# Low parts of the weights made by an accumulating transfer, and used last in a block's first tile and first in its last

## The chip, the cores and the metric

The kernel runs on one core of a Trainium2 chip. The metric is the time on the device in microseconds; lower is better. The engines of a core work side by side: TensorE (matrix products; PE in the profile, PEld for its weight loads), VectorE (DVE), ScalarE (ACT), GpSimd (POOL) and SyncE (SP, which here only issues transfers). Each runs its own instructions in order and waits for the others through semaphores. 16 DMA engines move data between device memory and the on-chip memory.

## The reference

The reference is a decoder trunk of two layers on one sequence of 512 positions with 1024 features, all in float32. A layer normalises x, projects it to all inputs of four mixers, runs the mixers, and adds their projected outputs to x:

```python
# for each of DEPTH = 2 layers, h: (512, 1024)
u = rmsnorm(h, norm_w[l])
z = u @ w_in[l]          # 1024 -> 15 blocks of 512 columns and 16 gate columns
mix = concat(retention(z), diff_attention(z), ssd(z), mlstm(z))   # 4 x 512
h = h + mix @ w_out[l]   # 2048 -> 1024
# at the end
out = rmsnorm(h, final_norm_w)
```

All mixers are causal and work in chunks of 128 positions. What they compute is not touched by the change; the projections' products are the same, the order of their terms in the sum is not.

## The kernel before, in words

**Two parts for each factor.** A product of float32 matrices is made of three products in a narrower format (`fp32r`). Each factor is split: the high part is the value cast to the narrower format, the low part is the value minus the high part. The kernel sums high*high, high*low and low*high. For the activations the parts are `uh` and `ul` (for a mixer's output `mh` and `ml`), for the weights `whi` and `wlo`.

**Tiles and blocks.** The input projection of a layer has 15 blocks of 512 columns, each with 8 pieces of 128 rows (k = 0 to 7). A block has four tiles; each fills one accumulator (`pspj`, of which there are two) with 8 x 3 = 24 matmuls. In `proj_tok` a tile is 128 positions, with the activations as the stationary factor; in `proj_feat` it is 128 features, with the weights stationary. The output projection `out_proj` handles a mixer's 512 rows at a time: two halves of 512 columns with 4 pieces of weights each, four tiles of 12 matmuls a half. A tile's matmuls go by k: the two with the high part of piece k, then the one with its low part.

**How the weights come in.** `split_w` loads two pieces at a time, a pair of 512 KB, into `raw` (two buffers) from SP's queue; `split_half` then casts each piece into `whi` on ScalarE and subtracts, into `wlo`, on GpSimd (pieces k = 0, 2, 4, 6, the tuple `POOL_K`) or on VectorE (the others). `whi` and `wlo` have ten buffers each, one piece a buffer, so a block and two pieces of the next fit. A buffer is free when the last matmul that reads it is done. The instructions of the split have a high priority on their engines (`W["hp"]`).

**Order.** A layer's steps come in this order:

```python
ORDER = ["mv", "gates", "mq", "mk", "mlstm", "mo", "mz", "dk", "dq", "diff", "dv", "dz", "m", "xs", "bc", "ssd", "d",
         "rqk", "sz", "rv", "rz", "ret", "s", "r"]
```

`m`, `d`, `s`, `r` are output projections, `gates`, `mlstm`, `diff`, `ssd`, `ret` the mixers, and all others blocks of the input projection. `gates` and the mixers run as tasks between the projections: `drive` takes the projection's matmuls one by one and, after each `yield`, issues the tasks that have come due on a clock of the TensorE time issued so far (`W` holds the delays). TensorE's order is written out in this way and kept. The other engines' instructions are ordered by a scheduler from priorities, except in the first block (`start`), whose order is written by hand and whose first tile has an order of its own for high and low parts as they come in.

**Around the projections.** A full accumulator is emptied by VectorE and ScalarE: convolution and SiLU (`ev_conv`, L476 to L483), rotation (`ev_rope`, L496 to L500, with a product on GpSimd), SiLU gates (`ev_silu`, L434 and L436), copies, and for the output projections the sum into `h` (L547). `rsqrt` runs on GpSimd (L207). `bcast` (L695) brings rows of the gates to all partitions by transfers from SP's queue. L115 is the line of all matmuls, L316 and L318 those of the cast and the subtraction, L323 that of the load into `raw`.

Of the kernel before, what the change touches and what calls it, by code (L numbers as in the profile page):

```python
# [28 lines left out]
# column offsets of the combined input projection  # L29
# [5 lines left out]
# the 512 column blocks in the order in which they are used  # L35
# [7 lines left out]
# columns of the row parameters that every partition gets  # L43
# [3 lines left out]
# the order of the steps of a layer  # L47
# [3 lines left out]
# the pieces of a block of weights whose low parts GpSimd computes  # L51
POOL_K = (0, 2, 4, 6)

# tiles that hold the queries' parts
QS = 4

# how much work of TensorE is issued before work that depends on other engines
# [5 lines left out]
# columns of the constants  # L63
# [31 lines left out]
class Trunk:  # L95
    def __init__(self, ctx, tc, aps, dbg=None):
        self.tc, self.nc = tc, tc.nc
        self.x, self.win, self.wg, self.wout, self.nrm, self.rows, self.convp, self.cst, self.out = aps
        self.dbg = dbg or {}
        mk = lambda n, b, **k: ctx.enter_context(tc.tile_pool(name=n, bufs=b, **k))  # L100
        self.cp = mk("cp", 1)
        self.pool = mk("pool", 1)
        self.ps = mk("ps", 2, space=bass.MemoryType.PSUM)
        self.n = 0
        # the order of TensorE's work: tasks come due on a clock of emitted TensorE time
        self.clk = 0.0
        self.heap = []
        self.done = set()
# [16 lines left out]
    def spawn(self, gen, delay=0.0):  # L125
        """Runs a generator; what it yields is the delay until it goes on."""
        def step():
            for w in gen:
                self.later(w, step)
                return  # L130
        self.later(delay, step)
# [44 lines left out]
    def setup(self):  # L176
        nc = self.nc
        self.h = [self.cp.tile([P, D], F32, name=f"h{t}") for t in range(NT)]
        for half in range(2):
            hs = slice(half * 512, (half + 1) * 512)  # L180
            nc.sync.dma_start(out=self.h[0][:, hs], in_=self.x[0:P, hs])
        self.load_nw(0, nc.sync)
        cst = self.cp.tile([P, C_W], F32, name="cst")
        nc.sync.dma_start(out=cst[:, 0:P], in_=self.cst[:, 0:P])
        self.rest = lambda: nc.sync.dma_start(out=cst[:, P:], in_=self.cst[:, P:])
        self.c = lambda o, w, p=P: cst[:p, o:o + w]
        self.ident = self.c(C_ID, P)
        self.ones = self.cp.tile([P, P], F32, name="ones")
        nc.vector.memset(self.ones, 1.0)
        # keeps TensorE busy until the first data come in, so that it runs at its full clock  # L190
        p = self.psum()
        for _ in range(12):
            self.mm(p[:, 0:P], lhsT=self.ones, rhs=self.ones)
        self.nhalf = self.cp.tile([P, 8], F32, name="nhalf")
        nc.vector.memset(self.nhalf, -0.5)
        self.zrow = self.cp.tile([4, P], F32, name="zrow")
        nc.vector.memset(self.zrow, 0.0)
# [35 lines left out]
    def load_nw(self, l, eng):  # L233
        """The weights of a norm of h, on every partition."""
        self.nw = [self.t("bcm", [P, 512], bufs=2) for _ in range(2)]
        for half in range(2):
            eng.dma_start(out=self.nw[half],
                          in_=self.nrm[l:l + 1, half * 512:(half + 1) * 512].to_broadcast([P, 512]))
# [72 lines left out]
    def split_half(self, raw, j, vector=False):  # L311
        nc = self.nc
        hi = self.t("whi", [P, 512], F32R, bufs=10)
        lo = self.t("wlo", [P, 512], F32R, bufs=10)
        with self.tc.high_priority(W["hp"]):
            (nc.vector.tensor_copy if vector else nc.scalar.copy)(out=hi, in_=raw)  # L316
            eng = nc.vector if j else nc.gpsimd
            eng.tensor_tensor(out=lo, in0=raw, in1=hi.bitcast(F32), op=ALU.subtract)  # L318
        return hi, lo

    def split_w(self, src, g):
        raw = self.t("raw", [P, 2, 512], bufs=2)
        self.nc.sync.dma_start(out=raw, in_=src)  # L323
        return [self.split_half(raw[:, j, :], 2 * g + j not in POOL_K) for j in range(2)]

    def load_block(self, name):
        b = BIDX[name]
        return [q for g in range(4) for q in self.split_w(self.win[self.l, b, :, 2 * g:2 * g + 2, :], g)]

    def start(self, evac):  # L330
        """The first block: the norm of x, and the weights, as they come in."""
# [9 lines left out]
        with self.tc.manual_schedule(engines={E.Activation, E.DVE, E.Pool, E.SP}):  # L341
# [3 lines left out]
            for k in range(KD):  # L345
                if k < 4:
                    if k % 2 == 0:
                        r = self.t("raw", [P, 2, 512], bufs=2)
                        nc.sync.dma_start(out=r, in_=self.win[0, b, :, k:k + 2, :])
                    raw.append(r[:, k % 2, :])  # L350
                else:
                    raw.append(self.t("z", [P, 512], bufs=8))
                    nc.sync.dma_start(out=raw[k], in_=self.win[0, b, :, k, :])
                if k == 3:
                    load(1)
# [4 lines left out]
            # on VectorE or GpSimd  # L360
            split = lambda k, v, h=False: w.append(self.split_half(raw[k], v, h))
            n = [self.norm_in_t(t) for t in range(NT)]
            # the products with the weights' high parts (0) and low parts (1), as these come in
# [32 lines left out]
    def proj_tok(self, name, evac, w=None, toks=range(NT), order=None):  # L396
        nc = self.nc
        w = w or self.load_block(name)
        for t in toks:
# [4 lines left out]
            for k, parts in order or [(k, (0, 1)) for k in range(KD)]:  # L404
                for part in parts:
                    for u in (self.uh,) if part else (self.uh, self.ul):
                        n += 1
                        self.mm(p, lhsT=u[:, k, ts_], rhs=w[k][part], start=(n == 1), stop=(n == 3 * KD))
                yield
# [3 lines left out]
    def proj_feat(self, name, evac):  # L413
        nc = self.nc
        w = self.load_block(name)
        for f in range(4):
            p = self.psum("pj")
            fs = slice(f * P, (f + 1) * P)
            for k in range(KD):
                hi, lo = w[k][0][:, fs], w[k][1][:, fs]  # L420
                self.mm(p, lhsT=hi, rhs=self.uh[:, k, :], start=(k == 0), stop=False)
                self.mm(p, lhsT=hi, rhs=self.ul[:, k, :], start=False, stop=False)
                self.mm(p, lhsT=lo, rhs=self.uh[:, k, :], start=False, stop=(k == KD - 1))
                yield
            evac(f, p)

    # evacuations
    def ev_silu(self, dst, tag, bufs, nwt=None):
        """2 * silu(z), times a row weight."""
# [57 lines left out]
    def ev_rope(self, sink, scale=1.0):  # L487
        """Rotates the heads' halves; the features lie on the partitions."""
# [21 lines left out]
    def finish_mix(self, mix):  # L510
        """Transposes of a mixer's output, in high and low parts, for the output projection."""
# [8 lines left out]
    def out_proj(self, g, mixt, tok_outer=False, after=None, cut=False, heads=False):  # L520
        nc = self.nc
        gi = GROUPS[g]
        w = [[x for q in range(2) for x in self.split_w(self.wout[self.l, gi, half, :, 2 * q:2 * q + 2, :], 2 * half + q)]
# [4 lines left out]
        for t, hf in order:  # L528
# [5 lines left out]
            for c0, c1 in zip(cuts, cuts[1:]):  # L534
# [4 lines left out]
                for k in range(4):  # L539
                    hi, lo = w[hf][k]  # L540
                    mh, ml = m(t, k)
                    self.mm(p, lhsT=mh, rhs=hi[:, cs], start=(k == 0), stop=False)
                    self.mm(p, lhsT=ml, rhs=hi[:, cs], start=False, stop=False)
                    self.mm(p, lhsT=mh, rhs=lo[:, cs], start=False, stop=(k == 3))
                    yield
# [15 lines left out]
    def gates(self):  # L561
# [20 lines left out]
        # log1p(exp(-|x|)) = 2 atanh(z / (2 + z)), z = exp(-|x|)  # L582
# [31 lines left out]
        # SSD factors  # L614
# [12 lines left out]
        # rows  # L627
# [19 lines left out]
        # running maxima: rows 0.. G, 32.. mu, 64.. G at the end of the chunk  # L647
# [44 lines left out]
    def bcast(self, src, n, t, tag, bufs):  # L692
        """Rows of src, columns of chunk t, on every partition."""
# [9 lines left out]
    def mlstm(self, v, th, zs, q, k, res):  # L703
# [5 lines left out]
        for t in range(NT):  # L709
# [47 lines left out]
            # denominators  # L757
# [18 lines left out]
            # r / 2 * rsqrt(r^2 / 4 * var + eps)  # L776
# [112 lines left out]
    def retention(self, qk, v, zs, res):  # L889
# [6 lines left out]
        for t in range(NT):  # L896
# [6 lines left out]
            # heads on different rows of the array write different banks  # L903
# [55 lines left out]
    def split_k(self, dst):  # L959
        """High and low parts of a head's keys, one above the other, for each of its two maps."""  # L960
# [13 lines left out]
    def split_q(self, x):  # L974
        """The high parts of a head's queries, on both halves of the partitions, and the low parts."""
# [108 lines left out]
    def layer(self, l, last):  # L1084
        """The steps of a layer that keep TensorE busy, and the mixers that run between them."""
# [40 lines left out]
        def end():  # L1126
# [7 lines left out]
            # mLSTM  # L1134
# [8 lines left out]
            # differential attention  # L1143
# [6 lines left out]
            # SSD  # L1150
# [5 lines left out]
            # retention  # L1156
# [7 lines left out]
    # columns of the last tokens' halves  # L1164
# [34 lines left out]
def _layout(i):  # L1199
    """The inputs, cut and reordered into the pieces that the kernel loads."""  # L1200
# [36 lines left out]
```

## Time and profile before

| what | value |
|---|---|
| runs | 1088.46, 1086.24, 1088.56 us; median 1088.46 |
| profiled execution, first to last instruction | 1091.0 us |
| TensorE matmuls | 1043.6 us busy (96%) |
| VectorE / ScalarE / GpSimd | 714.8 / 492.0 / 392.9 us busy |
| granted TensorE clock, mean | 0.984 |
| moved by the DMA engines | 95.53 MB, mean 88 GB/s |

The profile is of one execution; its span is 2.5 us longer than the median of the runs. A row of grouped instructions reads: line, engine, operation, output<-inputs, shapes, count, then busy us and mean ns of one, then the engine's idle time just before them and what ended it. A row of waits reads: who waited, for whom, us in total, times, longest. A row of transfers ends with the size of one and the median us from issue to landing. A row of the timeline reads: start, us, engine (q for its queue), line, operation, tiles, shapes, count, and in brackets the idle time before and what ended it. "Busy" of TensorE counts overlapping, pipelined matmuls once.

### The profile page before, as it was taken

Reading aid. Unit: us, or ns where it says so; the run is one execution under the profiler, and the core shown is the slowest. Engines: PE = TensorE matmul, PEld = TensorE weight load, DVE = VectorE, ACT = ScalarE, POOL = GpSimd, SP = SyncE. Lnnn points to the kernel's source line nnn. Section 1 sums busy time; section 2 is a strip of 40 time slices with the busy share of each in tenths; the row PEclk is TensorE's granted clock in tenths of the full one; section 3 lists DMA queues with packets and bytes.
Section 4 is the critical chain, followed back from the end, with each engine's and each line's share of the span. In section 5 each row is a group of like instructions: output and inputs, shape, how many; then the busy total and the mean of one; then the engine's idle time right before and its main releaser. Section 6 shows DMA issues by size and latency. Waiting matters only on the chain.

```text
span 1091.0 us, 14197 instructions
## 1 busy us (share of the span) xinstructions
PE 1043.6 (96%) x5052; PEld 848.7 (78%) x5052; DVE 714.8 (66%) x1369; ACT 492.0 (45%) x1082; POOL 392.9 (36%) x369
## 2 busy tenths in 40 slices
PE   7999989999999899999999999999999999999997
PEld 6778878777788787787887788787877877787776
DVE  5686676567787767445556867664687886773454
ACT  4444337655554344332344442484555542543332
POOL 3322445324323354225132234533252343542341
PEclk8999999999999999999999999899999999999999
DMA  7332313321312323332122322222231223223202
GB/s 283 102 100 85 97 49 97 96 77 57 92 46 79 106 68 97 108 119 72 39 82 74 116 89 86 78 77 77 79 101 55 78 87 107 71 85 115 78 20 77
DMA packets 39143, 95.53 MB, mean 88 GB/s; under 512 B 3592, under 2 KB 16520, under 8 KB 38944
## 3 DMA queue, kind: packets, MB, share of 16 engines
q1 hardware_dynamic: 38064, 93.18, 26.8%
q10 hardware_dynamic: 1008, 1.44, 0.4%
q8 instruction: 39, 0.64, 0.2%
q14 instruction: 32, 0.26, 0.1%
HBM read 92.47 MB, written 2.15 MB: 87 GB/s over the span
## 4 chain that ended last, share of the span: by engine, by line
PE 79%; DVE 11%; DMA 3%; issue 3%; ACT 3%; POOL 1%; SPq 0%; ACTq 0%; POOLq 0%; DVEq 0%
PE pspj L115 64%; PE psacc L115 6%; PE psS L115 5%; PE psS L119 4%; DVE wlo L318 3%; DMA raw<-in_w_in_dram 2%; DVE w L826 2%; DVE e L478 1%; ACT whi L316 1%; DMA cst<-in_consts_dram 1%; DVE w L721 0%; ACT e L496 0%; POOL s L207 0%; DVE z L436 0%; DVE ft L498 0%
## 5 line engine op out<-in xcount | busy, mean ns | idle before, releaser
L318 POOL TENSOR_TENSOR wlo<-raw,whi 128x512 fp32r<-128x512 f32 x150 | 206.5, 1380 | 358.8 <-ACT whi L316 231.7
L318 DVE TENSOR_TENSOR wlo<-raw,whi 128x512 fp32r<-128x512 f32 x150 | 173.7, 1159 | 89.4 <-ACT whi L316 76.9
L115 PE MATMUL pspj<-whi,uh 128*128 128x512 f32 x512 | 209.5, 409 | 8.5 <-DVE ft L498 8.2
L316 ACT CAST whi<-raw 128x512 fp32r<-128x512 f32 x300 | 175.8, 619 | 91.9 <-DMA raw<-in_w_in_dram 54.7
L115 PE MATMUL pspj<-whi,ul 128*128 128x512 f32 x512 | 201.8, 394 | 0.0
L115 PE MATMUL pspj<-wlo,uh 128*128 128x512 f32 x512 | 201.5, 395 | 0.2
L115 PE MATMUL pspj<-uh,whi 128*128 128x512 f32 x448 | 182.0, 406 | 9.3 <-DVE e L478 4.9
L115 PE MATMUL pspj<-uh,wlo 128*128 128x512 f32 x448 | 177.3, 396 | 1.2 <-POOL wlo L318 1.2
L115 PE MATMUL pspj<-ul,whi 128*128 128x512 f32 x448 | 176.4, 394 | 0.0
L115 PEld LDWEIGHTS pspj<-whi,uh 128*128 128x128 f32 x512 | 97.6, 191 | 31.0 <-DVE ft L498 9.7
L115 PE MATMUL pspj<-whi,mh 128*128 128x512 f32 (+1 forms) x260 | 107.4, 413 | 10.7 <-DVE h L547 8.0
L115 PEld LDWEIGHTS pspj<-wlo,uh 128*128 128x128 f32 x512 | 96.9, 190 | 22.7 <-DVE wlo L318 1.0
L115 PEld LDWEIGHTS pspj<-whi,ul 128*128 128x128 f32 x512 | 97.8, 191 | 18.2 <-DVE ul L306 0.2
L115 PEld LDWEIGHTS pspj<-uh,whi 128*128 128x128 f32 x448 | 85.6, 191 | 28.9 <-issue 6.1
L115 PE MATMUL pspj<-whi,ml 128*128 128x512 f32 (+1 forms) x260 | 102.2, 393 | 0.0
L115 PE MATMUL pspj<-wlo,mh 128*128 128x512 f32 (+1 forms) x260 | 102.2, 393 | 0.0
L115 PEld LDWEIGHTS pspj<-uh,wlo 128*128 128x128 f32 x448 | 85.4, 191 | 21.1 <-POOL wlo L318 2.5
L115 PEld LDWEIGHTS pspj<-ul,whi 128*128 128x128 f32 x448 | 85.6, 191 | 16.2
L207 POOL TENSOR_TENSOR s<-s,nhalf 128x4 f32<-128x4 f32 (+1 forms) x44 | 36.8, 837 | 160.2 <-DVE s L1058 76.0
L478 DVE SCALAR_TENSOR_TENSOR e<-pspj,cvh,e 128x511 f32<-128x511 f32 (+2 forms) x90 | 66.9, 744 | 14.6 <-ACT e L476 13.5
L115 PEld LDWEIGHTS pspj<-whi,mh 128*128 128x128 f32 x260 | 49.4, 190 | 23.7 <-DVE h L547 10.0
L496 ACT ACTIVATE e<-pspj 32x512 f32<-32x512 f32 x96 | 56.6, 590 | 12.9 <-PE pspj L115 11.4
(213 smaller groups left out, 1490.5 us busy)
## 6 DMA issues: line engine op xcount, KB each, us to landing
raw<-in_w_in_dram SPq DMA_DIRECT2D x118, 512.0 KB, 3.9
raw<-in_w_out_dram SPq DMA_DIRECT2D x32, 512.0 KB, 3.3
bcm<-adr SPq DMA_DIRECT2D x16, 256.0 KB, 3.4
bcm<-gdr SPq DMA_DIRECT2D x8, 256.0 KB, 4.9
out_dram<-z SPq DMA_DIRECT2D x7, 256.0 KB, 2.0
h<-in_x_dram SPq DMA_DIRECT2D x3, 512.0 KB, 8.5
rows<-in_rows_dram SPq DMA_DIRECT2D x2, 592.0 KB, 9.0
cst<-in_consts_dram SPq DMA_DIRECT2D x1, 1035.0 KB, 8.9
```

Source lines behind the costliest of these rows:

```text
L115: self.nc.tensor.matmul(out, lhsT=lhsT, rhs=rhs, start=start, stop=stop, **kw)
L119: self.nc.tensor.transpose(out, src, self.ident if ident is None else ident)
L207: self.nc.gpsimd.tensor_tensor(out=out, in0=m, in1=self.nhalf[:, :n], op=ALU.pow)
L316: (nc.vector.tensor_copy if vector else nc.scalar.copy)(out=hi, in_=raw)
L318: eng.tensor_tensor(out=lo, in0=raw, in1=hi.bitcast(F32), op=ALU.subtract)
L478: nc.vector.scalar_tensor_tensor(acc[:, s:], p[:, 0:S - s], w[:, 3 - s:4 - s], acc[:, s:], ALU.mult, ALU.add)
L496: nc.scalar.activation(x[q * 32:q * 32 + 32, :], p[o * 32:o * 32 + 32, :], AF.Copy, scale=scale)
L826: nc.vector.scalar_tensor_tensor(e[:, j * P:(j + 1) * P], ab[g][:, j, :], self.ncs[:, t, h:h + 1], self.cap, ALU.add, ALU.min)
```

## The change

Outside the first block, `split_w` makes both pieces of a pair at once, in tiles `whi` and `wlo` of two pieces with five buffers each (`WP`). ScalarE casts the pair into the high part in one instruction. VectorE no longer subtracts: it writes the negative of `raw`, in the narrower format, into `wlo`. Then GpSimd issues a transfer that reads the same weights from device memory a second time and adds them onto `wlo`. What results is the weights minus their value in the narrower format, the low part as before. GpSimd computes no low parts here any more.

The order of the terms changes in a block's first and last tile (for the output projections, in a half's): the first uses all high parts first and then all low parts, the last all low parts and then all high parts. The tiles between go piece by piece as before.

In the first block the split stays as it was (`split_half`, now writing into slices of pairs), and the first four pieces are loaded singly into buffers of another tag (`ft`) instead of in pairs into `raw`. All other lines of the diff remove comments.

```diff
-POOL_K = (0, 2, 4, 6)
+WP = 5, 5
+
+def parts(n, first, last):
+    hi, lo = [[(k, (j,)) for k in range(n)] for j in range(2)]
+    return hi + lo if first else lo + hi if last else [(k, (0, 1)) for k in range(n)]
...
-    def split_half(self, raw, j, vector=False):
-        nc = self.nc
-        hi = self.t("whi", [P, 512], F32R, bufs=10)
-        lo = self.t("wlo", [P, 512], F32R, bufs=10)
+    def pair(self):
+        return [self.t(tag, [P, 2, 512], F32R, bufs=n) for tag, n in zip(("whi", "wlo"), WP)]
+
+    def split_half(self, raw, hi, lo, j, vector=False):
+        nc = self.nc
         with self.tc.high_priority(W["hp"]):
             (nc.vector.tensor_copy if vector else nc.scalar.copy)(out=hi, in_=raw)
             eng = nc.vector if j else nc.gpsimd
             eng.tensor_tensor(out=lo, in0=raw, in1=hi.bitcast(F32), op=ALU.subtract)
         return hi, lo
 
-    def split_w(self, src, g):
+    def split_w(self, src):
+        nc = self.nc
         raw = self.t("raw", [P, 2, 512], bufs=2)
-        self.nc.sync.dma_start(out=raw, in_=src)
-        return [self.split_half(raw[:, j, :], 2 * g + j not in POOL_K) for j in range(2)]
+        nc.sync.dma_start(out=raw, in_=src)
+        hi, lo = self.pair()
+        with self.tc.high_priority(W["hp"]):
+            nc.scalar.copy(out=hi, in_=raw)
+            nc.vector.tensor_scalar(lo, raw, -1.0, None, ALU.mult)
+            nc.gpsimd.dma_start(out=lo, in_=src, accum_op=ALU.add)
+        return [(hi[:, j, :], lo[:, j, :]) for j in range(2)]
...
             for k in range(KD):
-                if k < 4:
-                    if k % 2 == 0:
-                        r = self.t("raw", [P, 2, 512], bufs=2)
-                        nc.sync.dma_start(out=r, in_=self.win[0, b, :, k:k + 2, :])
-                    raw.append(r[:, k % 2, :])
-                else:
-                    raw.append(self.t("z", [P, 512], bufs=8))
-                    nc.sync.dma_start(out=raw[k], in_=self.win[0, b, :, k, :])
+                raw.append(self.t("ft", [P, 512], bufs=11) if k < 4 else self.t("z", [P, 512], bufs=8))
+                nc.sync.dma_start(out=raw[k], in_=self.win[0, b, :, k, :])
...
+            pairs = [self.pair() for _ in range(4)]
+            split = lambda k, v, h=False: w.append(self.split_half(
+                raw[k], *[x[:, k % 2, :] for x in pairs[k // 2]], v, h))
...
     # proj_tok; proj_feat and out_proj (n = 4 pieces) likewise
-            for k, parts in order or [(k, (0, 1)) for k in range(KD)]:
-                for part in parts:
+            for k, ps in order or parts(KD, t == 0, t == NT - 1):
+                for part in ps:
                     for u in (self.uh,) if part else (self.uh, self.ul):
                         n += 1
                         self.mm(p, lhsT=u[:, k, ts_], rhs=w[k][part], start=(n == 1), stop=(n == 3 * KD))
                 yield
```

More of the change, by code (lines that the diff above doesn't have):

```diff
@@ L319, in split_half @@
         return hi, lo
-    def split_w(self, src, g):
+    def split_w(self, src):
+        nc = self.nc
         raw = self.t("raw", [P, 2, 512], bufs=2)
-        self.nc.sync.dma_start(out=raw, in_=src)
-        return [self.split_half(raw[:, j, :], 2 * g + j not in POOL_K) for j in range(2)]
+        nc.sync.dma_start(out=raw, in_=src)
[5 more added lines that the diff above has]
+        return [(hi[:, j, :], lo[:, j, :]) for j in range(2)]
     def load_block(self, name):
         b = BIDX[name]
-        return [q for g in range(4) for q in self.split_w(self.win[self.l, b, :, 2 * g:2 * g + 2, :], g)]
+        return [q for g in range(4) for q in self.split_w(self.win[self.l, b, :, 2 * g:2 * g + 2, :])]
     def start(self, evac):
@@ L359, in start @@
             self.loads(0)
-            split = lambda k, v, h=False: w.append(self.split_half(raw[k], v, h))
+            pairs = [self.pair() for _ in range(4)]
+            split = lambda k, v, h=False: w.append(self.split_half(
+                raw[k], *[x[:, k % 2, :] for x in pairs[k // 2]], v, h))
             n = [self.norm_in_t(t) for t in range(NT)]
@@ L418, in proj_feat @@
             fs = slice(f * P, (f + 1) * P)
[L419 to L423, printed above, removed]
+            n = 0
+            for k, ps in parts(KD, f == 0, f == 3):
+                for part in ps:
+                    for u in (self.uh,) if part else (self.uh, self.ul):
+                        n += 1
+                        self.mm(p, lhsT=w[k][part][:, fs], rhs=u[:, k, :], start=(n == 1), stop=(n == 3 * KD))
                 yield
@@ L522, in out_proj @@
         gi = GROUPS[g]
-        w = [[x for q in range(2) for x in self.split_w(self.wout[self.l, gi, half, :, 2 * q:2 * q + 2, :], 2 * half + q)]
+        w = [[x for q in range(2) for x in self.split_w(self.wout[self.l, gi, half, :, 2 * q:2 * q + 2, :])]
              for half in range(2)]
@@ L538, in out_proj @@
                 cs = slice(c0 - hf * 512, c1 - hf * 512)
[L539 to L544, printed above, removed]
+                n = 0
+                for k, ps in parts(4, t == 0, t == NT - 1):
+                    for part in ps:
+                        for x in m(t, k)[0:1] if part else m(t, k):
+                            n += 1
+                            self.mm(p, lhsT=x, rhs=w[hf][k][part][:, cs], start=(n == 1), stop=(n == 12))
                     yield
```

## The prediction

> **What bounds the kernel now.** I read the page first, then the waits of TensorE alone, then busy time by stretches.
>
> ```profile
> span 1091.0 us, 14197 instructions
> PE 1043.6 (96%) x5052; PEld 848.7 (78%) x5052; DVE 714.8 (66%) x1369; ACT 492.0 (45%) x1082; POOL 392.9 (36%) x369
> PE 79%; DVE 11%; DMA 3%; issue 3%; ACT 3%; POOL 1%; SPq 0%; ACTq 0%; POOLq 0%; DVEq 0%
> ```
>
> TensorE is busy in 1043.6 of 1091.0 us and carries 79% of the chain that ended last. The change keeps all its matmuls, so it can only move the 47 us of idle time, downwards by what it takes away, upwards without a limit. The waits of TensorE say what that idle time is:
>
> ```profile
> PE pspj L115 <- DVE ft L498: 8.7, 6, 2.2
> PE pspj L115 <- DVE h L547: 8.0, 5, 2.5
> PE pspj L115 <- DVE e L478: 4.9, 3, 2.3
> PE pspj L115 <- ACT whi L316: 4.3, 3, 2.0
> PE pspj L115 <- DVE z L436: 2.7, 2, 1.3
> PE psS L119 <- DVE w L884: 2.3, 2, 1.2
> PE pspj L115 <- POOL wlo L318: 1.2, 2, 0.6
> ```
>
> Waiting for the weights themselves costs 4.3 + 1.2 = 5.5 us. The larger part, about 27 us in these rows, is VectorE late with emptying the accumulators or with a mixer's step. VectorE is where a gain can come from; the weights are on time, and the question is by how much.
>
> **The change, part by part: engine time.**
>
> ```profile
> L318 POOL TENSOR_TENSOR wlo<-raw,whi 128x512 fp32r<-128x512 f32 x150 | 206.5, 1380 | 358.8 <-ACT whi L316 231.7 <-PE pspj L115 112.3 <-PE psS L115 13.8
> L318 DVE TENSOR_TENSOR wlo<-raw,whi 128x512 fp32r<-128x512 f32 x150 | 173.7, 1159 | 89.4 <-ACT whi L316 76.9 <-PE pspj L115 11.8
> L207 POOL TENSOR_TENSOR s<-s,nhalf 128x4 f32<-128x4 f32 (+1 forms) x44 | 36.8, 837 | 160.2 <-DVE s L1058 76.0 <-DVE s L227 45.7 <-DVE s L879 15.6
> L316 DVE CAST whi<-z 128x512 fp32r<-128x512 f32 x2 | 1.2, 661 | 0.0
> L1185 DVE TENSOR_SCALAR z<-z,s 128x512 f32<-128x512 f32 x1 | 0.5, 487 | 0.7 <-POOL s L207 0.7
> ```
>
> Outside the first block, 37 blocks of four pairs make 148 pairs. Removed: 148 subtractions on VectorE at 1.16 us (172 us) and 148 on GpSimd at 1.38 (204 us). Added on VectorE: 148 multiplications by -1 over 128x1024. The nearest row is L1185, the same operation on half the size, 0.49; the cast to fp32r takes 0.66 on that half size. So one costs 0.49 to 1.32 us; I take two of L1185, 0.97. VectorE saves 172 - 144 = 28 us, and its other instructions lose a neighbour. ScalarE casts the same bytes in 148 instructions instead of 296, no gain that TensorE sees. Of VectorE's lateness, h, z, w and about 4 us of ft lie outside the stretches considered below, 8.0 + 2.7 + 2.3 + 4 = 17 us; these waits have a mixer's chain behind them as well as weights, so I credit somewhat over half: **-10 us**. Between 0 and 17 is possible.
>
> **The path of the last pair.** Two raw buffers and five pairs of each part hold one block and one pair of the next. When a block follows a block, pairs 0 to 2 of the next are in raw or done, and the fourth raw load waits for a raw buffer. The last such boundary of layer 1 (rv to rz) shows it:
>
> ```profile
> 997.52 0.33 SPq L323 DMA_DIRECT2D raw<-in_w_in_dram  x1
> 1001.29 1.14 ACT L316 CAST whi<-raw 128x512 fp32r<-128x512 f32 x2 [0.85 <-DMA raw<-in_w_in_dram]
> 1002.47 1.36 DVE L318 TENSOR_TENSOR wlo<-raw,whi 128x512 fp32r<-128x512 f32 x1 [3.32 <-ACT whi L316]
> ```
>
> Issued 997.52, landed by 1001.29, last low part done at 1003.83. Today that is just in time. After the change the same chain gets a new start and a new end:
> - The last tile of the old block uses low parts first (8 matmuls), then high parts; its first pair of high parts is free after 12 of 24 matmuls. ScalarE then casts pair 1 of the new block into it (1.14 us, the double cast above) and only then is that raw buffer free for the fourth load. VectorE's multiplication, freed earlier, is not what holds it.
> - The fourth load lands, VectorE multiplies, GpSimd issues, the accumulating transfer lands.
> - The first tile of the new block needs that pair's low parts at its 23rd matmul.
>
> So what counts is the time from the 13th matmul of the old last tile to the 23rd of the new first tile. Busy time by stretches, TensorE alone, with exactly these ends, layer 1, in the order mq mk mo mz dk dq dv dz bc sz rv rz (columns: stretch, length, busy and count, granted clock, DMA share, GB/s):
>
> ```profile
> 570.62:583.29 12.67, 12.67 (x59) 1.00 0.54 160
> 598.31:609.24 10.93, 8.65 (x40) 1.00 0.44 139
> 624.26:631.97 7.71, 7.71 (x35) 1.00 0.45 139
> 653.54:663.54 10.00, 10.00 (x56) 1.00 0.58 178
> 684.97:696.41 11.44, 8.86 (x37) 0.92 0.29 92
> 713.83:722.08 8.25, 8.00 (x36) 1.00 0.40 127
> 736.13:747.91 11.78, 9.63 (x35) 0.86 0.42 126
> 764.40:773.96 9.56, 9.56 (x46) 1.00 0.44 141
> 855.46:865.28 9.82, 9.82 (x54) 1.00 0.52 154
> 944.59:952.40 7.81, 7.81 (x38) 1.00 0.45 136
> 972.76:981.03 8.27, 8.27 (x39) 1.00 0.43 129
> 996.93:1004.64 7.71, 7.71 (x36) 1.00 0.43 136
> sum 115.95, PE 108.69; mean PE 9.06
> ```
>
> The twelve of layer 0 sum to nearly the same:
>
> ```profile
> sum 117.12, PE 109.95; mean PE 9.16
> ```
>
> Against them stands the chain c. Its transfers:
>
> ```profile
> q1 hardware_dynamic: 38064, 93.18, 26.8%
> raw<-in_w_in_dram SPq DMA_DIRECT2D x118, 512.0 KB, 3.9
> raw<-in_w_out_dram SPq DMA_DIRECT2D x32, 512.0 KB, 3.3
> h<-in_x_dram SPq DMA_DIRECT2D x3, 512.0 KB, 8.5
> ```
>
> The load: 3.9. The accumulating transfer appears nowhere in the trace. It brings the same 512 KB and must also read what it adds to. 26.8% of 1091.0 us is 292 us for 93.18 MB, or 1.65 us of all engines per 512 KB; one more pass gives 3.9 + 1.65 = 5.5. Bounds: 3.3 (out weights, plain) and 8.5 (the same size behind other transfers); I take 5.5, nearest to the plain load of these very bytes. GpSimd's issue: at least what SP's costs (0.33, already inside the 3.9), at most GpSimd's smallest frequent work, L207's 0.84; I add the difference, 0.5. So c = 1.14 + 3.9 + 0.97 + 0.5 + 5.5 = **12.0 us**, between 1.14 + 3.9 + 0.49 + 0 + 3.3 = 8.8 and 1.14 + 3.9 + 1.32 + 0.84 + 8.5 = 15.7.
>
> Late by 12.0 minus the length, where positive: mk 1.1, mo 4.3, mz 2.0, dk 0.6, dq 3.8, dv 0.2, dz 2.4, bc 2.2, sz 4.2, rv 3.7, rz 4.3: 28.7 us a layer, twice that with layer 0 a little less, **+56 us**. TensorE's order is written out, so the mixers' matmuls behind the late one stand too. The high parts of that pair are less late (mo: cast done 1.14 + 3.9 + 1.14 = 6.2 after the stretch began, needed at the 13th matmul, 5.4), within the same stall. VectorE's waits inside stretches that bind, and the 5.5 us for the weights (dk), vanish into the new wait; nothing is credited for them.
>
> **The clock.** Three stretches hold an idle time over 2 us (length minus busy): mk, dk, dv. Their granted clock is 1.00, 0.92, 0.86: 0, 0.9 and 1.65 us lost, mean 0.86. Eight boundaries a layer get a stall of about 2 us or more: 16 x 0.86 = **+14 us**.
>
> **Costed at nothing.** Pairs 1 and 2: their raw data are there, low buffers come free from the third matmul of the old tile on, cover some 9 us against 7 needed (0.97 + 0.5 + 5.5); gone if transfers queue. Output projections: their halves are loaded ahead (only the third and fourth pair are late, for the second half). The first block: four 256 KB loads for two of 512 KB put two more issues of 0.33 on SP; below 1 us, either sign, since raw is free sooner. Twice as many scheduling points in first and last tiles: the mixers' matmuls shift by fractions of a us. GpSimd's queue: behind an issue that waits for VectorE stand the rope products (L499) and rsqrts (L207); today they stand behind subtractions that wait in the same way (231.7 us for ScalarE), so no new cost. On SP the broadcasts of the mixers' rows queue behind the fourth load, which comes about 0.6 us later than now (1.2 us behind the start of the stretch against 0.6, 997.52 against 996.93).
>
> Sum: 56 + 14 - 10 = +60 us. On the profiled execution 1091.0 + 60 = 1151; the median of the runs, 1088.46, lies 2.5 below that execution, so **1148 us**.
>
> **Rivals.**
> 1. Faster: the transfer is cheap and VectorE's relief counts in full. With c = 8.8 only mo, dq, sz, rv, rz bind, 4.2 us a layer, 8.5 in all, without a clock loss; VectorE's 17 us go, and inside the non-binding mk and dv its 2.3 + 2.1 us, twice: -26. Result 1088.5 - 17 = 1071. It decides while c stays under 9 (relief 10) to 10.4 (relief 26, stalls 28). For it: GpSimd's 204 us of two-input work leave the neighbourhood of VectorE. Against: c cannot go below two landings in series. The Trainium skill, DMA: Bandwidth & Descriptors, section Anatomy of one DMA, gives a transfer issued from GpSimd as 2.0 us plus bytes/436 GB/s, an estimate of 3.2 us for 512 KB, which would put c at about 9.7 and the time near this rival; the trace's plain 512 KB load, 3.9, is already above that figure. Chance 0.12.
> 2. Dear: the DMA engines become the bound of the boundaries. 148 transfers of two passes of 1.65 us add 488 us, 45% of the span, to 26.8%, in bursts of three around each boundary, with the fourth load among them. With landings of 8.5, c = 1.14 + 3.9 + 0.97 + 0.84 + 8.5 = 15.3: 67 us a layer, all 24 boundaries with a clock loss, 134 + 21 - 10 = +145, 1233 us. Against: even so the queues would be idle a quarter of the time. The Trainium skill, SBUF — State Buffer, section SBUF: two separate sides, adds another way to this end: VectorE in a mode that uses both ports keeps GpSimd from writing descriptors. No row here can show that. Chance 0.18.
> 3. Even: c near 9.5, relief near 15; the change does its work and nothing is left over, 1080 to 1114 us. Chance 0.08.
>
> **Numbers.** My forecast (c from 10.4 to 14, +26 to +114 us) has 0.62 and its own range 1114 to 1202. The range 1090 to 1230 leaves out rival 1, the lower part of 3 and the upper of 2. The runs before differ by 0.2%, which is what can be told from no change: faster 0.13, same 0.06, slower 0.81.
>
> **What would show it.** Right: TensorE's waits are led by the accumulating transfer into wlo at a first tile's last two low parts, 3 to 5 us each at mo, dq, sz, rv, rz in both layers, least at mq; the fourth load is issued about 1.2 us after a stretch's start (0.6 now); multiplication near 1 us; a lower granted clock behind the stalls; VectorE's waits for h and ft shorter. Wrong: an issue-to-landing time at or under 4 us, a fourth load that comes earlier than I trace it, or transfers that queue for 8 us and more.

## The result, and the profile after

| kernel | median of the runs, us | ratio (95% interval) |
|---|---|---|
| before | 1087.35 (1086.24 to 1088.56, 4 runs) | |
| after | 1408.82 (1401.24 to 1416.07, 4 runs) | 1.2935 (1.2869 to 1.3001) |

Here and for every run below, the ratio is to the kernel before, run beside it, and the bracket behind it is the 95% interval of that ratio.

Slower by 321 us. The forecast was 1148, and the range ended at 1230: the direction was right, the size was not. The page of the kernel after:

```profile
span 1414.3 us, 14019 instructions
PE 1152.9 (82%) x5052; PEld 921.0 (65%) x5052; DVE 616.6 (44%) x1369; ACT 472.3 (33%) x934; POOL 322.5 (23%) x369
q0 software_dynamic: 21312, 77.60, 30.8%
q1 hardware_dynamic: 38352, 93.18, 20.3%
PE 41%; DMA 28%; issue 14%; DVE 8%; ACT 4%; POOL 4%; SPq 0%; POOLq 0%; DVEq 0%; ACTq 0%
raw<-in_w_in_dram SPq DMA_DIRECT2D x116, 512.0 KB, 8.5
wlo<-in_w_in_dram POOLq DMA_DIRECT2D x116, 512.0 KB, 8.8
```

Span minus TensorE's busy time is 261.4 us, before 47.4: 214 of the 323 us (1414.3 against 1091.0) are idle time. The other 109 are busy time of the same 5052 matmuls, at a mean granted clock of 0.89 instead of 0.984. Transfers, 3% of the chain before, are 28% of it. The accumulating transfers are q0. The last two rows carry most of what follows: an accumulating transfer lands after 8.8 us, and the load into `raw`, which nobody changed, after 8.5 instead of 3.9.

TensorE's waits:

```profile
PE pspj L123 <- ACT whi L338: 106.5, 23, 6.6
PE pspj L123 <- DMA wlo<-in_w_in_dram: 103.4, 29, 6.1
PE pspj L123 <- DVE h L561: 16.3, 7, 5.2
```

Two waits of nearly equal size lead, not one. A first tile stops at its 13th matmul for the high part of the fourth pair, and again at its 23rd for the low part.

The prediction's last boundary (rv to rz, layer 1) in the timeline, rows chosen from the answers by engine:

```profile
1302.30 1.78 POOL L340 DMA_DIRECT2D wlo<-in_w_in_dram  x2 [21.00 <-DVE wlo L339]
1303.46 2.00 ACT L338 CAST whi<-raw 128x1024 fp32r<-128x1024 f32 x2 [2.13 <-PE pspj L123]
1304.54 0.33 SPq L335 DMA_DIRECT2D raw<-in_w_in_dram  x1
1305.49 10.19 SPq L335 DMA_DIRECT2D raw<-in_w_out_dram  x3
1313.26 2.07 ACT L338 CAST whi<-raw 128x1024 fp32r<-128x1024 f32 x2 [6.49 <-DMA raw<-in_w_in_dram]
1313.30 0.69 DVE L339 TENSOR_SCALAR wlo<-raw 128x1024 fp32r<-128x1024 f32 x1 [10.81 <-DMA raw<-in_w_in_dram]
1314.36 0.79 PE L123 MATMUL pspj<-whi,uh 128*128 128x512 f32 x1 [5.49 <-ACT whi L338]
1314.40 0.88 POOL L340 DMA_DIRECT2D wlo<-in_w_in_dram  x1 [10.32 <-DVE wlo L339]
1322.10 0.79 PE L123 MATMUL pspj<-wlo,uh 128*128 128x512 f32 x2 [3.11 <-DMA wlo<-in_w_in_dram]
```

Read it as the prediction's chain, from the 13th matmul of the old last tile (1303.26) to the 23rd of the new first one (1322.10):

| step | predicted us | measured us |
|---|---|---|
| until the fourth load is issued (the cast) | 1.14 | 1.28 (1304.54 - 1303.26) |
| fourth load, issue to landing | 3.9 | 8.72 (1313.26 - 1304.54) |
| VectorE's multiplication | 0.97 | 0.73 (to 1313.99, its start included) |
| until GpSimd's issue begins | 0 | 0.41 |
| issue and accumulating transfer | 0.5 + 5.5 | 7.70 (1322.10 - 1314.40) |
| sum | 12.0 | 18.84 |

Of the 6.8 us that the chain is longer than predicted, 4.8 are the plain load and 1.7 the accumulating transfer. Just ahead of the load two accumulating transfers were issued (1302.30, x2); beside the last accumulating transfer run the loads for the next weights (1305.49, x3, their issues spread over 10.19 us). The busy share of the DMA engines between 1300 and 1324, in 40 slices of 0.6 us and in tenths, shows them busy for most of the time or all of it from 1303.6 until shortly before the load lands at 1313.26:

```profile
DMA  0000009868999999999993000398959999999999
```

The same stretches as before, layer 1 (rows of mo, dq, sz and rz, then the sum of all twelve):

```profile
812.26:831.53 19.27, 10.24 (x35) 0.81 0.85 195
...
936.43:955.52 19.09, 10.23 (x35) 0.78 0.83 179
...
1232.40:1247.63 15.23, 9.75 (x36) 0.88 0.83 213
...
1303.26:1322.10 18.84, 10.24 (x35) 0.82 0.83 189
sum 228.38, PE 131.24; mean PE 10.94
```

and of layer 0:

```profile
sum 235.01, PE 129.25; mean PE 10.77
```

463.4 us instead of 233.1: 230 of the 323 us lie in these 24 short stretches, 188 of them idle and 42 in TensorE's busy time. Of the other 93, outside the stretches, 26 are idle and 67 busy time. The DMA engines are occupied to 0.83 to 0.85 in the four shown, against 0.40 to 0.45 in the same rows before.

### The profile page after: what moved, and what is told of

The parts are those of the page before. It is cut to its first block, busy times and chain, and to the rows that moved or that the text cites. A ratio compares the mean times of both kernels' runs of the same rounds, so it can differ in the third digit from the quotient of the medians.

```text
span 1414.3 us, 14019 instructions
## 1 busy us (share of the span) xinstructions
PE 1152.9 (82%) x5052; PEld 921.0 (65%) x5052; DVE 616.6 (44%) x1369; ACT 472.3 (33%) x934; POOL 322.5 (23%) x369
## 3 DMA queue, kind: packets, MB, share of 16 engines
q0 software_dynamic: 21312, 77.60, 30.8%
## 4 chain that ended last, share of the span: by engine, by line
PE 41%; DMA 28%; issue 14%; DVE 8%; ACT 4%; POOL 4%; SPq 0%; POOLq 0%; DVEq 0%; ACTq 0%
PE pspj L123 32%; DMA wlo<-in_w_in_dram 14%; DMA raw<-in_w_in_dram 10%; PE psacc L123 5%; DMA raw<-in_w_out_dram 3%; PE psS L123 3%; ACT whi L338 2%; PE psS L127 2%; DVE wlo L339 1%; POOL e L513 1%; POOL wlo L340 1%; DVE w L840 1%; ACT e L510 1%; DVE e L492 1%; DVE w L735 1%
## 5 line engine op out<-in xcount | busy, mean ns | idle before, releaser
L123 PE MATMUL pspj<-whi,uh 128*128 128x512 f32 x512 | 222.0, 434 | 67.4 <-ACT whi L338 66.2
L123 PE MATMUL pspj<-wlo,uh 128*128 128x512 f32 x512 | 192.9, 447 | 63.1 <-DMA wlo<-in_w_in_dram 63.1
L123 PE MATMUL pspj<-uh,whi 128*128 128x512 f32 x448 | 191.0, 426 | 41.9 <-ACT whi L338 40.3
L338 ACT CAST whi<-raw 128x1024 fp32r<-128x1024 f32 x148 | 151.3, 1045 | 220.9 <-DMA raw<-in_w_in_dram 140.0
L340 POOL DMA_DIRECT2D wlo<-in_w_in_dram x116 | 105.7, 962 | 497.8 <-DVE wlo L339 426.8
L123 PE MATMUL pspj<-whi,ul 128*128 128x512 f32 x512 | 213.4, 417 | 0.0
L339 DVE TENSOR_SCALAR wlo<-raw 128x1024 fp32r<-128x1024 f32 x148 | 101.5, 698 | 227.0 <-DMA raw<-in_w_in_dram 155.2
L123 PE MATMUL pspj<-uh,wlo 128*128 128x512 f32 x448 | 161.9, 435 | 40.4 <-DMA wlo<-in_w_in_dram 40.4
L123 PEld LDWEIGHTS pspj<-wlo,uh 128*128 128x128 f32 x512 | 109.7, 219 | 96.0 <-DMA wlo<-in_w_in_dram 71.7
L123 PEld LDWEIGHTS pspj<-whi,ul 128*128 128x128 f32 x512 | 104.7, 205 | 20.7 <-DVE ul L314 0.2
L123 PE MATMUL pspj<-whi,ml 128*128 128x512 f32 (+1 forms) x260 | 105.1, 405 | 0.0
L123 PE MATMUL pspj<-wlo,mh 128*128 128x512 f32 (+1 forms) x260 | 87.7, 405 | 0.4 <-DVE h L561 0.4
```

The costliest lines, as they stand in the source:

```text
L123: self.nc.tensor.matmul(out, lhsT=lhsT, rhs=rhs, start=start, stop=stop, **kw)
L338: nc.scalar.copy(out=hi, in_=raw)
L339: nc.vector.tensor_scalar(lo, raw, -1.0, None, ALU.mult)
L340: nc.gpsimd.dma_start(out=lo, in_=src, accum_op=ALU.add)
```

## The experiments

Theory: the transfers are in each other's way around a boundary, so that the fourth load and the last accumulating transfer each land late. Rivals: the order of the high and low parts costs the time by itself; or the engines' side of the change does; or most of it is the clock. The runs are told by the question they answer. Edits are to the kernel after unless another is named.

**Is it the second load, or the adding? (e1_plain)**

```diff
-            nc.gpsimd.dma_start(out=lo, in_=src, accum_op=ALU.add)
+            nc.gpsimd.dma_start(out=lo, in_=src)
```

> The second load is plain instead of accumulating: same bytes, same queue, same waits; the low parts then hold the weights themselves. Theory (the boundary chain, whose fourth raw load queues behind the two transfers that GpSimd has just issued, and whose last transfer shares the engines with raw loads): a plain transfer takes 1.65 us of all engines against 2.94 for an accumulating one, so the fourth load lands about 6.4 us after its issue (8.8 in the changed kernel), the last transfer after 5 to 6 (8.2): 1200 to 1300 us. Rival A (only adding in the transfer is dear, a second plain load is harmless): under 1130 us. Rival B (any transfer issued from GpSimd costs this, whatever it does): 1380 us or more.

1219.06 us, 1.1181 (1.1108 to 1.1253), within the theory's range. Its transfers and TensorE's waits:

```profile
q0 software_dynamic: 21312, 77.60, 20.1%
raw<-in_w_in_dram SPq DMA_DIRECT2D x116, 512.0 KB, 5.6
wlo<-in_w_in_dram POOLq DMA_DIRECT2D x116, 512.0 KB, 5.3
```

```profile
PE pspj L123 <- DMA wlo<-in_w_in_dram: 52.1, 26, 5.9
PE pspj L123 <- ACT whi L338: 41.6, 20, 3.9
```

Without the adding both waits fall, to 0.5 and 0.4 of what they were, and 190 us go, but 129 us over the kernel before in the runs beside it (1089.88) remain: the second copy of the weights costs a good part already. 148 transfers of 512 KB occupy 20.1% of 1222.4 us, 1.66 us of all engines each; with the adding, 30.8% of 1414.3 us, 2.94 each. The adding makes a transfer 1.77 times as expensive for the engines. VectorE's multiplications are the same in this run, so that VectorE keeps GpSimd from its work, rival 2's other way, does not by itself explain why the transfers land after 8.8 us instead of 5.3.

**With few bytes? (e2_small)**

```diff
-            nc.gpsimd.dma_start(out=lo, in_=src, accum_op=ALU.add)
+            nc.gpsimd.dma_start(out=lo[:, :, 0:16], in_=src[:, :, 0:16], accum_op=ALU.add)
```

> The accumulating transfer covers 16 columns of each piece instead of 512 (16 KB instead of 512 KB); the rest of the low parts stays the negative. All instructions, issues and waits stay. Theory (bytes on the shared engines): fourth load back to about 3.9 us, accumulating landing about 2.5 to 3.5 us, chain about 9 us, only mo, dq, sz, rv, rz late by 1 to 1.5 us, VectorE and GpSimd relieved: 1070 to 1095 us. Rival (GpSimd's issue, its in-order queue and the waits between ScalarE, VectorE, GpSimd and TensorE carry the loss, not the bytes): 1250 us or more.

1227.90 us, 1.1252 (1.1216 to 1.1287), far above what was expected.

```profile
q0 software_dynamic: 40256, 2.43, 6.0%
L340 POOL DMA_DIRECT2D wlo<-in_w_in_dram x116 | 142.1, 1225 | 441.4 <-DVE wlo L339 225.3
raw<-in_w_in_dram SPq DMA_DIRECT2D x116, 512.0 KB, 4.2
```

This was not the clean test that it was meant to be. One thirty-second of the bytes came as 40256 packets instead of 21312, and GpSimd's issue took 1225 ns instead of 962. It shows one thing: with so few bytes on the engines the plain load is back at 4.2. That the run is still slow goes in part with GpSimd: in its trace GpSimd stood for 164.4 us ahead of 48 of these issues without a wait that the profile shows, in the kernel after for 32.9 us ahead of 38, and 60.8 us of TensorE's waits are for these small transfers. What holds GpSimd there stays open.

**No accumulating transfer at all (x_none).** The low parts stay the negatives that VectorE writes; order, casts and VectorE's work are those of the change.

```diff
-            nc.gpsimd.dma_start(out=lo, in_=src, accum_op=ALU.add)
```

> The changed kernel without any accumulating transfer: the low parts stay the negatives that VectorE writes, all else as in the changed kernel. Theory (the fourth raw load is late because it stands behind the accumulating transfers; what then remains is the order, which lets high parts go late and wants them early, each stall followed by a slower clock): fourth load about 4 us, TensorE's waits for whi about 30 us in place of 106, none for wlo, 1110 to 1150 us. Rival A (the order is harmless once the transfers are gone): 1070 to 1095 us. Rival B (the waits of ScalarE, VectorE and SyncE on each other in the new split carry the late high parts): waits for whi 80 us or more, over 1200 us.

1087.06 us, 0.9969 (0.9951 to 0.9987): the loss is gone, as rival A had it and not the theory. Its plain loads, TensorE's wait for the high parts, and its twelve stretches, layer 1 and then layer 0:

```profile
raw<-in_w_in_dram SPq DMA_DIRECT2D x116, 512.0 KB, 4.4
PE pspj L123 <- ACT whi L338: 20.7, 16, 2.3
```

```profile
sum 123.24, PE 111.24; mean PE 9.27
```

```profile
sum 119.05, PE 108.56; mean PE 9.05
```

TensorE is busy for 1038.5 us at a clock of 0.992, so the new order does not lengthen the matmuls by itself; the 1152.9 of the kernel after come with the stalls.

**Which transfers make which wait? (x_first_last, x_not_last)** The pairs that keep the accumulating transfer are chosen by their number in the block; the others keep the negatives.

```diff
-            nc.gpsimd.dma_start(out=lo, in_=src, accum_op=ALU.add)
+            if g in (0, 3):      # x_not_last: (0, 1, 2)
+                nc.gpsimd.dma_start(out=lo, in_=src, accum_op=ALU.add)
```

> Accumulating transfers only for the first and the last pair of each block (for output projections the first and the last of its four); those of the two middle pairs, which are issued just ahead of the fourth raw load, are left out, so their low parts stay the negatives. Theory (queueing behind those two): the fourth raw load lands in about 4 us instead of 8.8, waits for whi near 30 us, waits for wlo stay at 80 to 110 us: 1250 to 1310 us. Rival (the fourth load is late for another reason than the two transfers ahead): waits for whi 80 us or more, 1370 us or more.

> Accumulating transfers for the first three pairs of each block, none for the last, whose low part stays the negative. Theory: the fourth raw load still stands behind two transfers and lands in 8 to 9 us, waits for whi stay at 90 to 110 us, waits for wlo nearly vanish: 1230 to 1290 us. Rival (the late high parts come from the last pair's own transfer, or from raw loads of the next block): waits for whi under 50 us, under 1180 us.

x_first_last, 1300.33 us, 1.1944 (1.1863 to 1.2025), in the theory's range, though its wait for low parts is longer than expected; its waits and its plain loads:

```profile
PE pspj L123 <- DMA wlo<-in_w_in_dram: 145.4, 29, 8.1
PE pspj L123 <- ACT whi L338: 16.5, 17, 2.3
```

```profile
raw<-in_w_in_dram SPq DMA_DIRECT2D x116, 512.0 KB, 4.8
```

x_not_last, 1247.33 us, 1.1457 (1.1416 to 1.1498), in the theory's range:

```profile
PE pspj L123 <- ACT whi L338: 105.1, 23, 6.8
PE pspj L123 <- DMA wlo<-in_w_in_dram: 0.8, 1, 0.8
```

```profile
raw<-in_w_in_dram SPq DMA_DIRECT2D x116, 512.0 KB, 7.8
```

This is the clearest pair of the study. Take away the transfers of pairs 1 and 2, which no tile waits for, and the plain load falls from 8.5 to 4.8 and the wait for the high parts from 106.5 to 16.5. Keep those and take away the fourth pair's own, and the wait for the high parts stays at 105.1 while the wait for low parts is down to 0.8. So the wait at the 13th matmul is the fourth load behind the transfers of pairs 1 and 2: 160 us on x_none's 1087 with next to no wait for an accumulating transfer. The fourth pair's own transfer comes on top: the kernel after takes 162 us more than x_not_last. Where the load is not late, in x_first_last, it costs 213 us over x_none; 160 and 213 are more than the 322 of both together, so the two costs overlap.

**Is it the order? (e3_order_only, e4_by_piece)** e3_order_only is the kernel before with `parts` and the three loops that use it, as in the change; the split stays as it was. e4_by_piece is the kernel after with

```diff
-    return hi + lo if first else lo + hi if last else [(k, (0, 1)) for k in range(n)]
+    return [(k, (0, 1)) for k in range(n)]
```

> The kernel before with only the order of terms in first and last tiles changed; low parts by subtraction on VectorE and GpSimd. Theory: the last pair's high parts come about 0.6 us later and are wanted up to 1.4 us earlier, the fourth load takes 3.9 us, so at most about 1 us of stall at the shortest boundaries: 1085 to 1110 us. Rival (the later release of the high parts is what makes TensorE wait 106 us for ScalarE in the changed kernel): 1180 us or more.

> The changed kernel with all tiles by piece as before, the accumulating transfers kept. Theory: the chain is the same, buffers come free earlier by about 1.4 us, but the low parts of pairs 1 and 2 are wanted before their transfers land, and the fourth load still queues: 1350 to 1450 us, the waits now mostly for wlo. Rival (the new order delays the fourth load and is most of the loss): under 1250 us.

e3_order_only: 1168.18 us, 1.0709 (1.0679 to 1.0738), 78 us over the kernel before in the runs beside it (1089.88) and far above what was expected.

```profile
PE pspj L119 <- ACT whi L320: 58.6, 19, 5.7
```

All high parts first means that the fourth pair's are needed at the 13th matmul of the first tile, not at the 19th. These 78 us are not a share of the 321, though. The trace at rv to rz shows the fourth load issued 2.4 us after the 13th matmul of the old last tile (1068.79 against 1066.42), since here a raw buffer is free only after the subtractions, which wait for the casts, and these for the high buffers; in x_none, where the multiplication waits for no cast, it is 1.3 us (991.88 against 990.61), in the kernel before 0.6.

e4_by_piece: 1327.93 us, 1.2179 (1.2086 to 1.2273), between the theory's range and the rival's, 81 us under the kernel after; its waits for weights are nearly all for low parts:

```profile
PE pspj L123 <- DMA wlo<-in_w_in_dram: 144.6, 65, 6.5
PE pspj L123 <- DMA wlo<-in_w_out_dram: 28.8, 8, 5.5
```

So the order does not earn the slack that it gives the low parts; it takes more from the high parts. But most of the loss, 238 us over the kernel before in the runs beside it, is there without it.

**What are the engines' savings worth? (x_none_by_piece)** x_none with e4_by_piece's edit: no transfers and no new order.

> The changed kernel without any accumulating transfer and with all tiles by piece as before; the low parts stay the negatives. This is the relief of VectorE and GpSimd by itself. Theory (the relief is real, some 10 to 25 us, and was hidden in the run without transfers by the 21 us that the new order makes TensorE wait for whi): 1060 to 1078 us. Rival (the relief is nothing, TensorE's waits for VectorE have other causes): 1083 to 1092 us.

1069.30 us, 0.9805 (0.9777 to 0.9833), as expected. The relief is about 20 us, and about the most that such transfers could gain here. Against x_none it shows the order's price where no transfer is in the way: 18 us.

**Is it the clock? (e7_warm, e7b_warm128)** Fourteen matmuls with a stationary factor of zeros before the 13th and 23rd matmul of the first tile, in eleven kinds of blocks of both layers, 616 in all; they add zero. In e7_warm the zeros have 4 rows, in e7b_warm128 128. The lines of e7b_warm128, without those that make the zeros (`z`) and call this at each matmul (`n`):

```diff
...
+        if first and name in ("mk", "mo", "mz", "dk", "dq", "dv", "dz", "bc", "sz", "rv", "rz") and n in (12, 22):
+            for _ in range(14):
+                self.nc.tensor.matmul(p, lhsT=z, rhs=rhs, start=False, stop=False)
```

> The changed kernel with 14 matmuls whose stationary factor is zero (they add nothing to the accumulator) put into the first tile of mk, mo, mz, dk, dq, dv, dz, bc, sz, rv and rz ahead of its 13th and of its 23rd matmul, where TensorE stands still; 3.2 us each at full clock, 141 us in all, inside the waits. Theory (after each stall the clock is granted at half for some us, and this slows the real matmuls by about 100 us in all): clock lost falls by half or more, 1300 to 1370 us although matmuls are added. Rival (the clock loss lies in the waits and costs nothing): 1400 to 1440 us.

> As the run with 14 zero matmuls ahead of the 13th and the 23rd matmul, but with a stationary factor of 128 rows of zeros and a moving one of 128 rows (there: 4 rows). The 4-row fills left the granted clock at 0.89 while TensorE was issuing. Theory (the clock follows how much of the array works; 128 rows keep it up, and the slow clock behind the stalls is worth some 100 us): clock above 0.94, 1300 to 1390 us. Rival (zeros do not count either, or the clock loss costs nothing): clock 0.88 to 0.90, 1405 to 1440 us.

e7_warm: 1427.19 us, 1.3109 (1.3015 to 1.3203), at a granted clock of 0.887. The time is in the rival's range, but the clock did not rise, so this run says nothing about its price. e7b_warm128: 1383.78 us, 1.2695 (1.2611 to 1.2778), clock 0.951, both as expected; the page's engines, and the fills among the groups by line:

```profile
PE 1236.3 (90%) x5668; PEld 995.6 (72%) x5668; DVE 615.0 (45%) x1369; ACT 472.7 (34%) x934; POOL 323.8 (24%) x369
```

```profile
L414 PE MATMUL pspj<-whi,zz 128*128 128x512 f32 x392 | 94.3, 392 | 0.0
L414 PE MATMUL pspj<-uh,zz 128*128 128x512 f32 x224 | 55.1, 398 | 0.0
```

1236.3 less 149.4 leaves 1086.9 us for the real matmuls, against 1152.9: 66 of the 109 us of added busy time go with the higher clock. The time falls by only 25 us: the fills stand in TensorE's order, and where a stall is shorter than their 14 x 0.39 = 5.5 us they can lengthen it. In x_none, where the stalls are gone, the clock is at 0.992: its loss comes with the stalls and is no cause beside them.

**Could a version gain? (h1_by_piece, e8_all_dve)** h1_by_piece: by piece, and only the first pair of a block by an accumulating transfer, the others subtracted.

```diff
+        if g not in (0,):
+            for j in range(2):
+                self.split_half(raw[:, j, :], hi[:, j, :], lo[:, j, :], j)
+            return [(hi[:, j, :], lo[:, j, :]) for j in range(2)]
```

> A version meant to win: the accumulating transfer only for the first pair of each block, which is loaded a block ahead; the other pairs are subtracted on GpSimd and VectorE as before, tiles by piece as before. Theory (a transfer far from the boundary costs nothing, a quarter of the relief stays): 1078 to 1090 us. Rival (any accumulating transfer stands in the way of raw loads that matter, and pairs as release unit cost more than pieces): 1095 us or more.

1109.03 us, 1.0175 (1.0141 to 1.0209), the rival's range. Its transfers from the input weights (eight more are from the output weights):

```profile
wlo<-in_w_in_dram POOLq DMA_DIRECT2D x29, 512.0 KB, 7.6
```

None of TensorE's waits is for them. Buffers that come free in pairs, and the transfers themselves, are not told apart here; this stays open.

e8_all_dve takes up what x_none_by_piece leaves: the kernel before with nothing changed but that GpSimd subtracts nothing.

```diff
-POOL_K = (0, 2, 4, 6)
+POOL_K = ()
```

> The kernel before with all low parts outside the first block subtracted on VectorE, none on GpSimd: is it GpSimd beside it that makes VectorE late? VectorE's subtraction is 0.68 us where GpSimd is idle and 1.36 beside it, so 296 x 0.68 = 201 us against 174 now. Theory (VectorE's amount of work sets its lateness): 1088 to 1105 us. Rival (the neighbour sets it): under 1082 us.

1067.43 us, 0.9805 (0.9773 to 0.9837): faster than both kernels, by the rival's reading and not by mine.

```profile
PE 1031.6 (97%) x5052; PEld 842.1 (79%) x5052; DVE 707.0 (67%) x1517; ACT 491.6 (46%) x1082; POOL 191.4 (18%) x221
L318 DVE TENSOR_TENSOR wlo<-raw,whi 128x512 fp32r<-128x512 f32 x298 | 212.6, 741 | 65.6 <-ACT whi L316 64.0
```

VectorE does 148 subtractions more and is still busy for less: 707.0 us against 714.8. One subtraction takes 741 ns on average instead of 1159, so all of them take 212.6 us instead of 173.7. That is 39 us more, so the rest of VectorE's work must have become over 40 us shorter; the rotation's L500, for one, falls from 1041 to 689 ns. The Trainium skill, SBUF — State Buffer, section Who interferes with whom, says that a VectorE instruction with two inputs in SBUF contends with a GpSimd instruction that reads SBUF; the subtraction and L500 have two such inputs, and the means agree with it and give the size.

## Why the prediction was wrong, and where it was right

Right: the chain and where it lies; but it brought two stalls where the prediction saw one. The chain runs through the cast, the fourth load, the multiplication, the issue and the transfer, in that order, and it starts 1.28 us into the stretch (1.2 predicted). The rule "late by the chain minus the stretch" holds: with a chain of 18.84 in place of 12.0 it gives 12 x 18.84 - 115.95 = 110 us for layer 1 and 109 for layer 0, 219 in all, where 230 were measured. As the 18.84 comes from one of these stretches, the better support is that 20 of the 24 now last between 18.8 and 20.9 us, whether they took 7.7 or 12.7 before. Pairs 1 and 2 stayed covered: x_not_last waits 0.8 us for low parts. The price of the transfer was near the best case. The answer for its line, over all transfers:

```profile
DMA to landing us min/median/max: 5.4/8.6/11.5
```

The fastest took 5.4 from the start of its issue; the prediction had 0.5 + 5.5. With only one such transfer a block, in h1_by_piece, the fastest took 6.3 and the median 7.6, so even there 6.0 was short. The 3.2 us by the Trainium skill, DMA: Bandwidth & Descriptors, section Anatomy of one DMA, lie below all of them, and below the fastest plain load from GpSimd in e1_plain, 3.5.

Wrong, by the prediction's own steps:

- **"The load: 3.9."** 8.7, worth 4.8 of the chain's 6.8 us. This is the step that failed most. The 3.9 was the median of a trace without accumulating transfers, and the prediction kept it at both ends of its bounds for c, although it took 8.5, "the same size behind other transfers", as the upper bound of the accumulating transfer. The change itself puts two accumulating transfers just ahead of this load: 2 x 2.94 + 1.65 = 7.5 us of all engines until it is through. x_first_last without these two has 4.8. The Trainium skill, DMA: Bandwidth & Descriptors, section Queues, rings and completion order, has an engine take turns between queues packet by packet. Between 1300 and 1324 q1 moved 2.10 MB in 567 packets and q0 1.95 MB in 526, so a load and an accumulating transfer of 512 KB have about equally many. If each packet of the load waited for one of the others, the load would wait for one of the two transfers only: 1.65 + 2.94 = 4.6 us on the engines, and with the 2.25 that a load alone takes beyond its 1.65, an estimate of 6.8. The median of 8.5 is above it, so this count of turns does not explain the whole delay; how the engines shared their time between the two queues stays open.
- **"I take 5.5"** for the last transfer, with 0.5 for its issue: 7.7, worth 1.7 us. The next weights' loads share the engines with it, but since h1_by_piece has 7.6 as well, how much of the 1.7 is theirs is not shown. Rival 2 had just this, "landings of 8.5" and the engines as the bound of the boundaries, but for the accumulating transfer alone; the plain load in the same chain kept its 3.9, and so the rival stopped at 1233.
- **"The high parts of that pair are less late", "within the same stall".** They became a stall of their own, 106.5 us in all, at the 13th matmul. Both the late load and the new order lead there; x_none, with the order and without any transfer, has 20.7 of it.
- **The order, costed only through the start of the chain.** It costs 78 us in the subtracting kernel, 81 in the changed one, and 18 in the changed one without transfers.
- **The clock, +14.** TensorE's busy time grew by 109 us; 66 of them went in e7b_warm128, where the clock rose. The prediction lost clock at 16 boundaries; the kernel after stands still for over 3.6 us at each of the 24, and the stretches in the rows above run at 0.78 to 0.88.
- **VectorE's relief, -10.** About 20 without transfers and new order. In the kernel after the wait for `ft` vanished, but TensorE's wait for `h` went from 8.0 to 16.3 us, although the prediction looked for a shorter one. A likely reason is that the multiplication stands in VectorE's queue until its load lands (10.81 us in the timeline above), and what empties the accumulators stands behind it; in x_none, where loads land after 4.4 us, the wait for `h` is 5.0, and in x_not_last, with 7.8, it is 16.0. But e4_by_piece has 6.3 with loads of 7.6, so the order has a part in it, and the reason is not shown by a run of its own. The prediction named what queues behind GpSimd and SP, not this.

## What to carry to other kernels

A transfer's time in the trace of before is its time in that company: before pricing a chain, list what the change itself puts in flight ahead of and beside each transfer in it, and add their engine time, also to the transfers that the diff does not touch. An order that gives one operand slack takes it from another; work out for both at which matmul each is needed. And before work is moved from an engine to transfers, try what is gained by merely not sharing: here one line, with GpSimd's subtractions given to VectorE, brought the 2% that is about the best that the transfers could have gained.

## What the runs showed of the hardware

- An accumulating transfer of 512 KB occupies the DMA engines for 2.94 us of all sixteen, a plain one for 1.66; it landed in 5.4 us at best, after 7.6 (median) where there was one a block, and after 8.8 in the kernel after.
- With half of the subtractions on GpSimd one of VectorE's took 1159 ns on average, with nearly all on VectorE 741. VectorE's other instructions became shorter as well, by over 40 us in all, so that it was less busy with twice as many subtractions.
- Zero matmuls of 4 rows during a stall left the granted clock at 0.887 (0.89 without them); with 128 rows it was 0.951.
- VectorE's multiplication of 128x1024 with a cast to fp32r took 698 ns, less than twice the 487 of half its size in plain float32:

```profile
L339 DVE TENSOR_SCALAR wlo<-raw 128x1024 fp32r<-128x1024 f32 x148 | 101.5, 698 | 227.0 <-DMA raw<-in_w_in_dram 155.2
```
